# Splitting the first store of a rotary-embedding kernel: 2 KB rows first, then 30 KB rows

## Chip, cores, metric

One core of one Trainium2 chip. The metric is the device time in microseconds of that core.

## The reference

`x` is float32 of shape (8, 8, 1024, 64); `positions` has 1024 entries, `freqs` 32, `scale` is 0.5.

```python
half = x.shape[-1] // 2
angles = np.outer(positions * scale, freqs)
cos, sin = np.cos(angles), np.sin(angles)
x_first, x_second = x[..., :half], x[..., half:]
out = concatenate([x_first * cos - x_second * sin,
                   x_first * sin + x_second * cos], axis=-1)   # float32
```

Input and output are 16.8 MB each, and each is moved once.

## The kernel before

x is cut into NU = 4 units of 4 MB, each laid out as 128 partitions with one row of 32 KB (N = 8192 float32) in DRAM. GpSimd's DMA queue loads them with a cast to fp16, except for half of unit 0, of which Sync's and ScalarE's queues load a quarter each as float32. (In the code P = 128, NH = 4096 is half a row and Q = 2048 a quarter.) VectorE multiplies in fp16, ScalarE casts back to float32 into OUT, and the result is stored: units 0 and 1 in one 4 MB store each on GpSimd's queue, units 2 and 3 in halves on Sync's queue.

```python
xout = ctx.enter_context(tc.tile_pool(name="xout", bufs=3))
X0f = xout.tile([P, N], FP32, tag="O")
pin(nc.sync.dma_start(out=X0f[:, :Q], in_=xv[0][:, NH : NH + Q]))
# ... positions, freqs and the other quarter of unit 0 on the scalar queue (cut)
pin(nc.gpsimd.dma_start(out=Xf[0][:, :NH], in_=xv[0][:, :NH]))      # cast to fp16
# ... constants (cut)
for u in range(1, NU):
    pin(nc.gpsimd.dma_start(out=Xf[u], in_=xv[u]))                  # cast to fp16
# ... sin/cos tables: T (cut)
for u in range(NU):
    OUT = xout.tile([P, N], FP32, tag="O")
    for s in range(2):
        # ... ks, ns, sin_b, cos_b, pr (cut)
        pin(nc.vector.tensor_tensor(out=pr, in0=Xs, in1=sin_b, op=ALU.mult))
        pin(nc.vector.tensor_tensor(out=Xs, in0=Xs, in1=cos_b, op=ALU.mult))
        # ... subtract into the first half, add into the second half (cut)
        pin(nc.scalar.copy(out=OUT[:, ns], in_=Xf[u][:, ns]))
        if u >= NU // 2:
            pin(nc.sync.dma_start(out=ov[u][:, ns], in_=OUT[:, ns]))
    if u < NU // 2:
        pin(nc.gpsimd.dma_start(out=ov[u], in_=OUT))
```

Of the kernel before, what the change touches and what calls it, by code (L numbers as in the profile page):

```python
# [21 lines left out]
def kernel(  # L22
# [8 lines left out]
    nc = tc.nc  # L31
    pin = tc.keep_in_program_order
# [12 lines left out]
    K8 = S // P  # L45
    G = P // HP
    W = K8 * half
    assert S % HP == 0 and D == 2 * half and NBH % HEADS == 0 and G * K8 == K

    fscale = float(scale)  # L50
# [2 lines left out]
    ov = out.rearrange("b h s d -> (b h s d)").rearrange("(u p n) -> u p n", p=P, n=N)  # L53
# [34 lines left out]
        out=one, in_=one, compare_op=ALU.not_equal, fill=1.0, base=0,  # L88
        pattern=[[-1, G], [-G, HP]], channel_multiplier=1,
    ))  # L90
    for u in range(1, NU):
# [9 lines left out]
        out=posf, in_=pos_i64.bitcast(I32).rearrange("p (k t) -> p k t", t=2)[:, :, 0]  # L101
# [3 lines left out]
        out=y,  # L105
# [8 lines left out]
        out=r, in0=m, scalar=_MAGIC, in1=y, op0=ALU.subtract, op1=ALU.subtract  # L114
# [5 lines left out]
        out=ra.bitcast(I32), in0=r.bitcast(I32), scalar1=0x7FFFFFFF, scalar2=None, op0=ALU.bitwise_and  # L120
# [5 lines left out]
    for g in range(0, G, 2):  # L126
        ps = spread.tile([P, 2, 2, W], FP32, tag="g")
        for i in range(2):
            nc.tensor.matmul(  # L129
                out=ps[:, i].rearrange("p t w -> p (t w)"),  # L130
# [12 lines left out]
# [3 lines that stand above are left out]
            ks = slice(s * KH, (s + 1) * KH)  # L146
            ns = slice(s * NH, (s + 1) * NH)
            Xs = X[u][:, ks]
            sin_b = T[:, 0, ks].unsqueeze(2).broadcast_to((P, KH, 2, half))
            cos_b = T[:, 1, ks].unsqueeze(2).broadcast_to((P, KH, 2, half))  # L150
            pr = tmp.tile([P, KH, 2, half], FP16, tag="pr")
            pin(nc.vector.tensor_tensor(out=pr, in0=Xs, in1=sin_b, op=ALU.mult))  # L152
            pin(nc.vector.tensor_tensor(out=Xs, in0=Xs, in1=cos_b, op=ALU.mult))  # L153
            pin(nc.vector.tensor_tensor(  # L154
                out=Xs[:, :, 0, :], in0=Xs[:, :, 0, :], in1=pr[:, :, 1, :], op=ALU.subtract
            ))
            pin(nc.vector.tensor_tensor(  # L157
                out=Xs[:, :, 1, :], in0=pr[:, :, 0, :], in1=Xs[:, :, 1, :], op=ALU.add
            ))
            pin(nc.scalar.copy(out=OUT[:, ns], in_=Xf[u][:, ns]))  # L160
            if u >= NU // 2:
                pin(nc.sync.dma_start(out=ov[u][:, ns], in_=OUT[:, ns]))
        if u < NU // 2:
            pin(nc.gpsimd.dma_start(out=ov[u], in_=OUT))  # L164


# [33 lines left out]
```

## Time and profile before

| | before |
|---|---|
| time, median (lowest to highest, 6 runs) | 84.56 us (84.42 to 84.83) |
| span in the profile | 82.8 us |
| VectorE / ScalarE busy | 60.3 us / 40.1 us |
| bytes read and written in HBM | 16.79 + 16.78 MB |
| first DMA row to end of the last one | 79.76 us |

The utilisation slices and the chain of the kernel before are shown in the prediction.

One quantity is used throughout and is on no page. The trace keeps a record of each row that an engine moves (start, duration, bytes). A cast load row of 32 KB has a record of 1.227 us in the steady state. The **hole** is what the records of the load rows exceed their usual duration by, ahead of the first store row, as a mean over the 16 engines: 0.96 us before.

### The profile page before, as it was taken

To read this page: it belongs to the slowest core of one execution; us is meant where nothing else is said; L and a number is where in the kernel's file an instruction comes from. 1 tells how busy PE (TensorE), PEld (TensorE's weight loads), DVE (VectorE), ACT (ScalarE), POOL (GpSimd) and SP (SyncE) were. 2 spreads that over 40 slices of the span, in tenths; PEclk is the share of its full clock that TensorE was granted. 3 is DMA by queue.
4 is the path that set the end of the run, shared out by engine and by line. 5 is a ranking of instruction groups with operands and counts; after the bars stand their busy time and mean duration, and the time that the engine had idled before them with its cause. 6 is when DMAs were issued, how large, how long until landed. Compare 5 with 4: busy or idle time off the path is not lost.

```text
span 82.8 us, 179 instructions
## 1 busy us (share of the span) xinstructions
PE 7.0 (8%) x18; PEld 2.7 (3%) x18; DVE 60.3 (73%) x40; ACT 40.1 (49%) x18; POOL 4.6 (6%) x14
## 2 busy tenths in 40 slices
PE   0011799200000000000000000000000000000000
PEld 0011233000000000000000000000000000000000
DVE  0306276999999999999999999999999997000000
ACT  0602159999960690294088049209606912950000
POOL 4920000000000002000000200000000000000000
PEclk9999999975555555555555555555555555555555
DMA  2899998997999899699979989999899999999991
GB/s 40 335 326 269 293 333 182 253 238 150 246 253 198 182 253 238 143 253 253 127 301 459 507 348 412 507 443 420 380 436 420 412 420 436 444 420 436 428 428 55
DMA packets 1874, 26.22 MB, mean 317 GB/s; under 512 B 338, under 2 KB 338, under 8 KB 338
## 3 DMA queue, kind: packets, MB, share of 16 engines
q0 software_dynamic: 864, 15.73, 66.4%
q1 hardware_dynamic: 720, 9.44, 27.2%
q10 hardware_dynamic: 290, 1.06, 3.2%
HBM read 16.79 MB, written 16.78 MB: 406 GB/s over the span
## 4 chain that ended last, share of the span: by engine, by line
DVE 55%; ACT 14%; issue 6%; DMA 6%; PE 5%; DVEq 1%; ACTq 0%
DVE pr L152 19%; DVE X L153 19%; DVE X L157 9%; DVE X L154 6%; DMA freq_row<-in_freqs_dram 6%; ACT T L139 5%; ACT OUT L160 4%; PE ps L129 4%; ACT X L140 4%; DVEq L195 1%; PE cfreq L97 1%; ACT tab L122 1%; DVE r L113 1%; DVE y L104 1%; ACTq L69 0%
## 5 line engine op out<-in xcount | busy, mean ns | idle before, releaser
L160 ACT CAST OUT<-X 128x4096 f32<-128x4096 f16 x8 | 28.8, 3606 | 24.2 <-DVE X L157 24.2
L152 DVE TENSOR_TENSOR pr<-X,T 128x4096 f16<-128x4096 f16 x8 | 18.3, 2292 | 1.0 <-ACT T L139 0.7
L153 DVE TENSOR_TENSOR X<-X,T 128x4096 f16<-128x4096 f16 x8 | 18.3, 2292 | 0.3
L154 DVE TENSOR_TENSOR X<-X,pr 128x2048 f16<-128x2048 f16 x8 | 9.8, 1225 | 0.3
L157 DVE TENSOR_TENSOR X<-pr,X 128x2048 f16<-128x2048 f16 x8 | 9.7, 1219 | 0.0
L139 ACT CAST T<-ps 128x1024 f16<-128x1024 f32 x6 | 5.7, 1030 | 2.6 <-PE ps L129 2.6
L129 PE MATMUL ps<-tab,sel 128*128 128x512 f16 x16 | 6.4, 584 | 2.2 <-ACT tab L122 2.2
L137 DVE CAST T<-ps 128x1024 f16<-128x1024 f32 x2 | 2.5, 1225 | 2.2 <-PE ps L129 2.2
L140 ACT CAST X<-X0f 128x4096 f16<-128x4096 f32 x1 | 3.7, 3651 | 0.0
L164 POOL DMA_DIRECT2D out_dram<-OUT x2 | 1.1, 536 | 40.3 <-ACT OUT L160 40.3
L95 DVE COPY sel<-one 128x2048 f16<-128x2048 f16 x1 | 0.7, 693 | 2.8 <-POOL one L87 2.8
L117 ACT ACTIVATE tab<-r 128x256 f16<-128x256 f32 x1 | 0.4, 416 | 4.3 <-DVE r L113 4.3
L129 PEld LDWEIGHTS <-sel 128*128 128x128 f16 x16 | 2.2, 138 | 6.0 <-issue 5.8
L117 ACT ACT_TABLE_LOAD x1 | 1.3, 1283 | 2.1 <-issue 2.1
L92 POOL DMA_DIRECT2D X<-in_x_dram x3 | 2.0, 658 | 0.0
L100 DVE CAST posf<-pos_i 128x8 f32<-128x8 int32 x1 | 0.2, 172 | 2.3 <-DMA pos_i<-in_positions_dram 2.3
L97 PE MATMUL cfreq<-freq_row,coef 1*128 1x32 f32 x2 | 0.6, 392 | 5.9 <-DMA freq_row<-in_freqs_dram 5.9
L104 DVE TENSOR_TENSOR y<-posf,cfreq 128x256 f32<-128x256 f32 x1 | 0.4, 422 | 0.5 <-PE cfreq L97 0.5
L83 POOL DMA_DIRECT2D X<-in_x_dram x1 | 0.7, 667 | 0.8 <-POOLq L181 0.8
L97 PEld LDWEIGHTS cfreq<-freq_row,coef 1*128 1x128 f32 x2 | 0.5, 305 | 5.8 <-issue 5.8
L122 ACT ACTIVATE tab<-ra,quarter 128x256 f16<-128x256 f32 x1 | 0.5, 507 | 0.0
L113 DVE SCALAR_TENSOR_TENSOR r<-m,y 128x256 f32<-128x256 f32 x1 | 0.4, 424 | 0.0
(10 smaller groups left out, 1.9 us busy)
## 6 DMA issues: line engine op xcount, KB each, us to landing
out_dram<-OUT POOLq DMA_DIRECT2D x2, 4096.0 KB, 20.8
out_dram<-OUT SPq DMA_DIRECT2D x4, 2048.0 KB, 11.6
X<-in_x_dram POOLq DMA_DIRECT2D x3, 2048.0 KB, 28.7
X0f<-in_x_dram SPq DMA_DIRECT2D x1, 1024.0 KB, 4.8
X<-in_x_dram POOLq DMA_DIRECT2D x1, 1024.0 KB, 11.7
X0f<-in_x_dram ACTq DMA_DIRECT2D x1, 1024.0 KB, 12.2
pos_i<-in_positions_dram ACTq DMA_DIRECT2D x1, 8.0 KB, 5.0
freq_row<-in_freqs_dram ACTq DMA_DIRECT2D x1, 0.1 KB
```

Of the source, the lines that this page charges most:

```text
L92: pin(nc.gpsimd.dma_start(out=Xf[u], in_=xv[u]))
L97: nc.tensor.matmul(out=cfreq, lhsT=coef, rhs=freq_row, start=True, stop=True)
L117: pin(nc.scalar.activation(out=tab[:, 0], in_=r, func=AF.Sin, bias=0.0, scale=-_TWO_PI_DN))
L129: nc.tensor.matmul(out=ps[:, i].rearrange("p t w -> p (t w)"), lhsT=sel[:, g + i].rearrange("s h q -> s (h q)"), rhs=tab.rearrange("s t k ...
L137: pin(nc.vector.tensor_copy(out=dst, in_=ps))
L139: pin(nc.scalar.copy(out=dst, in_=ps))
L140: pin(nc.scalar.copy(out=Xf[0][:, NH:], in_=X0f[:, :NH]))
L152: pin(nc.vector.tensor_tensor(out=pr, in0=Xs, in1=sin_b, op=ALU.mult))
L153: pin(nc.vector.tensor_tensor(out=Xs, in0=Xs, in1=cos_b, op=ALU.mult))
L154: pin(nc.vector.tensor_tensor(out=Xs[:, :, 0, :], in0=Xs[:, :, 0, :], in1=pr[:, :, 1, :], op=ALU.subtract))
L157: pin(nc.vector.tensor_tensor(out=Xs[:, :, 1, :], in0=pr[:, :, 0, :], in1=Xs[:, :, 1, :], op=ALU.add))
L160: pin(nc.scalar.copy(out=OUT[:, ns], in_=Xf[u][:, ns]))
```

## The change

The intent: let small rows be the first that are stored, when GpSimd's queue passes from loads to stores.

```diff
+    C1 = 512
...
         if u < NU // 2:
-            pin(nc.gpsimd.dma_start(out=ov[u], in_=OUT))
+            c = C1 if u == 0 else 0
+            if c:
+                pin(nc.gpsimd.dma_start(out=ov[u][:, :c], in_=OUT[:, :c]))
+            pin(nc.gpsimd.dma_start(out=ov[u][:, c:], in_=OUT[:, c:]))
```

## The prediction

> **What bounds the kernel now.** I read the page from the utilisation slices to the queues, and only then the chain that ended last, because the two disagree. The chain names VectorE and ScalarE; the slices say that the 16 DMA engines are never free:
>
> ```profile
> span 82.8 us, 179 instructions
> DVE  0306276999999999999999999999999997000000
> ACT  0602159999960690294088049209606912950000
> DMA  2899998997999899699979989999899999999991
> HBM read 16.79 MB, written 16.78 MB: 406 GB/s over the span
> DVE 55%; ACT 14%; issue 6%; DMA 6%; PE 5%; DVEq 1%; ACTq 0%
> ```
>
> VectorE is done in slice 34 of 40 and ScalarE in slice 36, but DMA runs at nine tenths to the last slice but one. The few sevens and sixes come from the way a row is booked in the slice in which it starts. 33.6 MB in 82.8 us is close to all that these engines give here, as the stretches show (us, busy time of five engines with counts, clock, DMA share, GB/s):
>
> ```profile
> 26.00:38.00 12.00, 0.00 (x0) 0.00 (x0) 11.83 (x8) 6.99 (x2) 0.54 (x1) 0.50 1.02 217
> 38.00:39.00 1.00, 0.00 (x0) 0.00 (x0) 1.00 (x1) 0.22 (x1) 0.00 (x0) 0.50 0.91 164
> 39.00:40.00 1.00, 0.00 (x0) 0.00 (x0) 0.97 (x2) 0.00 (x0) 0.00 (x0) 0.50 0.57 115
> 40.00:41.00 1.00, 0.00 (x0) 0.00 (x0) 1.00 (x2) 0.00 (x0) 0.00 (x0) 0.50 2.01 262
> 41.00:42.00 1.00, 0.00 (x0) 0.00 (x0) 0.97 (x2) 0.34 (x1) 0.00 (x0) 0.50 0.00 0
> 42.00:43.00 1.00, 0.00 (x0) 0.00 (x0) 1.00 (x1) 1.00 (x1) 0.00 (x0) 0.50 1.25 524
> 43.00:55.00 12.00, 0.00 (x0) 0.00 (x0) 11.83 (x8) 5.87 (x2) 0.53 (x1) 0.50 1.01 437
> 67.00:79.00 12.00, 0.00 (x0) 0.00 (x0) 2.78 (x3) 3.60 (x1) 0.00 (x0) 0.50 1.01 431
> ```
>
> Until about 40 us the queue loads x with a cast (217 GB/s of fp16 written means twice that read, 434); from 42 us it stores at 431 to 437. Both are the same ceiling, reached from the read side and then from the write side. The only hole is between them: no row starts between 41 and 42 us. The trace's records of single rows (a row is one partition's run; each engine moves 8 rows of a DMA) size it. Cast rows of 32 KB start every 1.209 us on an engine, averaged over the 16. The last two of unit 3 take 1.412 us (38.993 to 40.405) and 1.991 us (40.405 to 42.396, where the first store row starts). Their excess is 0.20 + 0.78 = 0.98 us, or 0.96 without the 0.02 us of a completion record. Between the loads of two units there is no such excess (20.830 to 22.059 is 1.229, completion record included), nor between the two 4 MB stores (50.875 to 52.090). After 42.05 us the records of one engine add up to 39.05 us and the last ends at 81.50: no more idle time. So a delay removed at the turn is a delay removed at the end.
>
> What stands next behind DMA is the last store. The chain in order of time ends, and the DMA queue's own waits read:
>
> ```profile
> 69.84 3.60 ACT OUT L160
> SPq L162 <- ACT OUT L160: 71.3, 4, 51.2
> SPq L195 <- DMA out_dram<-OUT: 7.6, 2, 4.8
> ```
>
> Its copy ends at 73.44 and its last row is recorded as moved at 81.49; it has landed at 81.86, and the span closes 0.9 us later. On idle DMA it would need about 1.0 us to start (the first load is issued at 0.74, its first row starts at 1.74), eight rows of 0.611 us each, 4.89 us, and 0.37 us from last row to landing: 73.5 + 1.0 + 4.9 + 0.4 = 79.8. So 2.1 us can be taken from DMA before compute sets the end.
>
> **What the Trainium skill says.** "DMA: Bandwidth & Descriptors", section "Issuing engines are not separate DMA queues": all DMAs, whoever issues them, run on the same 16 engines and interleave. The trace agrees: from 55.8 us rows of the GpSimd queue (1.213 us) and the Sync queue (0.611 us) alternate, and the sum stays at the ceiling. The same page, section "Measured (HBM→SBUF, 128 partitions, SWDGE, issued from GpSimd)", has 425 GB/s for 16 MB; the stretches here show 431 to 437. Its section "Latency and other measured facts" gives HBM access 0.2 us on average and 2 us at high load; a hole of 0.96 us lies between, but no view shows the latency itself. "Perfetto Trace Analysis", section "DMA Optimizations": DMAs below 2 KB have a significant overhead each, and splitting helps if the engines are generally idle. Here they are not idle, and 2 KB is the edge.
>
> **The change, part by part.**
> *Removed*: one GpSimd store of 128 rows of 32 KB (unit 0). *Added*: a store of 128 rows of 2 KB, 256 KB in all, and one of 128 rows of 30 KB. Bytes are the same. The 2 KB store reads columns of the first half only, so it waits for one copy and can be issued at 20.40 + 3.61 = 24.0 us instead of 31.5. This moves nothing: GpSimd's queue works in order, all three unit loads were put on it by 4.7 us, and they end at 42. Instruction order on VectorE, ScalarE, TensorE and Sync is the same in both builds; one copy of the last unit now waits for three DMAs instead of two, the new one long landed by then (unit 0's store lands at 52.7, that copy starts at 62.84).
> *Cost of the rows*: the records give 309, 611 and 1213 ns for 8, 16 and 32 KB, so 36.7 ns per KB and about 9 ns per row. Estimated from that, a 2 KB row takes 82 ns, a 30 KB row 1.14 us; eight of each make 0.66 + 9.12 = 9.78 us on an engine against 8 x 1.213 = 9.70. With one more completion record (0.009 us) the cost is +0.09 us, all on the path. GpSimd's further issue, 0.54 us, is off it: the descriptors are written at 24 to 32 us and used at 42.
> *Gain at the turn*: only the 0.96 us hole is there to be won. My reading of it: an engine reads ahead of what it writes. During loads the read side is the limit, so when it begins on the store's 32 KB rows before the load has ended, those bytes delay the load's last rows: 0.96 us x 27 KB per us is about 26 KB per engine, most of one row. If the engine takes in whole rows by number, small first rows let it take in little (two or three would be 4 to 6 KB, 0.15 to 0.22 us), and 0.7 to 0.8 us is saved; it stays saved, since reads and writes run at one rate afterwards. If it takes in bytes, eight rows of 2 KB are only 16 KB per engine, and it reads on into the 30 KB row: nothing is saved.
>
> The trace speaks rather for bytes, or for many rows. The Sync store is issued at 52.33; with 1.0 us to start it could move at 53.3, but its first row starts between 55.8 and about 57.2, some 2.4 us (two 32 KB rows, 64 KB) beyond the rest of a row in work. At the start, GpSimd's load is issued at 1.25, yet its first row starts at 4.79, after the last of Sync's 8 KB rows: there at least six small rows were already in hand. So I expect part of the hole at best.
>
> **The rivals.**
> 1. *Whole rows by number*: gain 0.7 to 0.8, less 0.09: 83.8 to 83.9. For it: the hole is nearly a row long, and lies just where this change acts. Against: the eight small rows in hand at the start.
> 2. *Bytes, or a fixed latency of turning from HBM reads to stores*: gain 0, cost 0.09: 84.6. For it: 64 KB in hand in both cases above.
> 3. *In between*: the read-ahead stops at the 16 KB of small rows, since a 30 KB row no longer fits; 26 - 16 = 10 KB, 0.36 us saved, less 0.09: 84.25.
> 4. *Small rows are slower than the fit*, or a second, shorter hole opens when reading turns to 30 KB rows: 0.2 to 0.5 us lost, 84.7 to 85.0. For it: the skill's warning on small DMAs; no row near 2 KB is in this trace.
> A compute-set end is no rival: 2.1 us of room against 0.96.
>
> **Range and chances.** Weights 0.35, 0.3, 0.2 and 0.15 on 83.85, 84.6, 84.25 and 84.85 give 84.3; I put 84.2, as one seldom writes such an edit without a hole in view. The range is rival 1 at its fullest with the runs' noise (84.42 to 84.83 before), 83.5, to rival 4, 84.8. Faster by 2% needs 1.69 us, more than the hole holds: 0.03. Slower by 2% needs eight small rows to cost 0.2 us more each: 0.02.
>
> **What would show it.** In the changed profile the stretch 40 to 43 us tells: under rival 1 the last two load rows take close to 1.21 us each and the first store row starts near 41.6; under rival 2 they take 1.4 and 2.0 as before and the first store row starts near 42.4. The small rows should take 80 to 90 ns, the 30 KB rows 1.14 us, and no gap should follow. From there the engines' work should add up to 39.1 us and run without idle time to the end; the time should move by what the start of the first store row moved, plus 0.09. VectorE and ScalarE should show the same times as before to 0.1 us. The prediction is wrong if the end moves without that start moving, if a new hole lies between the two stores, or if the end comes below 79.8 us in the trace.

## The result, and the profile after

84.56 us median (84.49 to 84.82, 6 runs), against 84.56 us before (84.42 to 84.83, 6 runs). The ratio is 1.0002, 95% interval 0.9978 to 1.0026: the same. Ratios here are the mean time of one kernel's runs over the mean of the other's of the same rounds, so they are not quite the ratio of the medians quoted. Executions over 1.5% slower than the fastest of the same kernel are left out of the means.

From the page of the changed kernel, the lines that answer to those of before, and three lines of its DMA issues (KB each, median us from issue to landing):

```profile
span 82.8 us, 181 instructions
...
DVE  0306376999999999999999999999999996000000
ACT  0603069999950790393097059119507903930000
...
DMA  3899997997999899799989999999999899999990
...
HBM read 16.79 MB, written 16.78 MB: 405 GB/s over the span
...
out_dram<-OUT POOLq DMA_DIRECT2D x1, 4096.0 KB, 20.8
out_dram<-OUT POOLq DMA_DIRECT2D x1, 3840.0 KB, 21.5
out_dram<-OUT POOLq DMA_DIRECT2D x1, 256.0 KB, 19.6
```

The small store takes 19.6 us to land for 256 KB: it was issued at 24.1 us and stood behind the loads until 42, as predicted. Now the stretches of the changed kernel around the turn (us; busy time of five engines with counts; clock; DMA share, which can pass 1 because a row is booked whole where it starts; GB/s):

```profile
26.00:38.00 12.00, 0.00 (x0) 0.00 (x0) 11.83 (x8) 7.18 (x2) 0.53 (x1) 0.50 1.02 217
38.00:39.00 1.00, 0.00 (x0) 0.00 (x0) 1.00 (x1) 0.03 (x1) 0.00 (x0) 0.50 0.85 147
39.00:40.00 1.00, 0.00 (x0) 0.00 (x0) 0.97 (x2) 0.00 (x0) 0.00 (x0) 0.50 0.67 131
40.00:41.00 1.00, 0.00 (x0) 0.00 (x0) 1.00 (x2) 0.00 (x0) 0.00 (x0) 0.50 1.93 262
41.00:42.00 1.00, 0.00 (x0) 0.00 (x0) 0.97 (x2) 0.53 (x1) 0.00 (x0) 0.50 0.01 4
42.00:43.00 1.00, 0.00 (x0) 0.00 (x0) 1.00 (x1) 1.00 (x1) 0.00 (x0) 0.50 1.25 514
...
43.00:55.00 12.00, 0.00 (x0) 0.00 (x0) 11.83 (x8) 5.68 (x2) 0.53 (x1) 0.50 1.01 437
```

The empty microsecond from 41 to 42 us is still there (4 GB/s against 0), and 437 GB/s follow at once. In the records: the last two load rows take 1.44 and 1.93 us, a hole of 0.92 us against 0.96; the store begins at 42.34 us on the mean of the engines, 42.40 before. After the turn, the records of an engine add up to 39.09 us against 39.05. So the change removed nothing and cost next to nothing.

### The profile page after: what moved, and what is told of

It is laid out like the page before. It is cut to its first block, busy times and chain, and to the rows that moved or that the text cites. A ratio compares the mean times of both kernels' runs of the same rounds, so it can differ in the third digit from the quotient of the medians.

```text
span 82.8 us, 181 instructions
## 1 busy us (share of the span) xinstructions
PE 6.8 (8%) x18; PEld 2.7 (3%) x18; DVE 60.3 (73%) x40; ACT 40.1 (48%) x18; POOL 5.2 (6%) x15
## 4 chain that ended last, share of the span: by engine, by line
DVE 55%; ACT 15%; issue 6%; DMA 5%; PE 5%; DVEq 1%; ACTq 0%
DVE X L154 19%; DVE pr L153 19%; DVE X L158 9%; DVE X L155 6%; DMA freq_row<-in_freqs_dram 5%; ACT T L140 5%; ACT OUT L161 4%; PE ps L130 4%; ACT X L141 4%; DVEq L199 1%; PE cfreq L98 1%; ACT tab L123 1%; DVE r L114 1%; DVE y L105 1%; ACTq L70 0%
## 5 line engine op out<-in xcount | busy, mean ns | idle before, releaser
L168 POOL DMA_DIRECT2D out_dram<-OUT x2 | 1.1, 532 | 20.2 <-ACT OUT L161 20.2
L167 POOL DMA_DIRECT2D out_dram<-OUT x1 | 0.6, 554 | 19.4 <-ACT OUT L161 19.4
## 6 DMA issues: line engine op xcount, KB each, us to landing
out_dram<-OUT POOLq DMA_DIRECT2D x1, 256.0 KB, 19.6
```

## The experiments

The question is why the hole does not care about the size of the rows, and what it is. Theories, as they came:

- **Rows by number**: an engine takes in a few rows ahead; small rows would shrink the hole.
- **Bytes read ahead because loads with a cast leave the write side idle** (the prediction's reading).
- **Fixed turn**: each turn from loads to stores costs about 0.96 us.
- **First touch**: the first write to the output costs it, once.
- **Lead**: reading from SBUF gets ahead of the loads still under way, once, and the pipeline keeps that lead until it runs empty.

Medians of "before" below are those of the same chip and rounds. Each hole is read from one trace.

### small4: four stores of 2 KB rows instead of one

```diff
-            pin(nc.gpsimd.dma_start(out=ov[u], in_=OUT))
+            edges = [0, 512, 1024, 1536, 2048, N] if u == 0 else [0, N]
+            for lo, hi in zip(edges, edges[1:]):
+                pin(nc.gpsimd.dma_start(out=ov[u][:, lo:hi], in_=OUT[:, lo:hi]))
```

> Unit 0's store as four stores of 2 KB rows (64 KB per engine) and one of 24 KB rows. The hole at the turn was 0.98 us before and 0.92 us after the change (excess of the last two load rows over 1.209 us, completion record included). Theory 'rows by number' (some 9 to 15 rows taken in ahead, so that eight small ones were too few): the hole shrinks below 0.5 us. Theory 'bytes' (about 26 KB per engine taken in ahead): it stays at 0.85 to 1.0, as 64 KB of small rows lie behind it. Theory 'fixed turn': stays too. Small rows 2 x 2 KB in one record of 159 ns as in the changed kernel, so the work after the turn grows by about 4 x 0.03 us; time within 0.3% of before unless the hole shrinks.

84.44 us (before 84.57), ratio 0.9973 (0.9930 to 1.0015): the same. The hole is 0.77 us. That is a little below the 0.85 that "bytes" expected and far from the 0.5 of "rows by number"; since single traces of kernels without small rows spread from 0.81 to 1.23 us (split_x3 0.81, sync_store0 0.84, before 0.96, two_turns 1.01, less_dve 1.23), nothing is read from the 0.08. 64 KB per engine in small rows leave the hole standing: rows by number falls.

### split_x3 and two_turns: does each turn cost?

split_x3 loads unit 3 in two halves, order unchanged. two_turns puts the second half behind unit 0's store, so that the queue turns to stores twice:

```diff
-        pin(nc.gpsimd.dma_start(out=Xf[u], in_=xv[u]))
+        if u < NU - 1:
+            pin(nc.gpsimd.dma_start(out=Xf[u], in_=xv[u]))
+        else:
+            pin(nc.gpsimd.dma_start(out=Xf[u][:, :NH], in_=xv[u][:, :NH]))
...
             pin(nc.gpsimd.dma_start(out=ov[u], in_=OUT))
+            if u == 0:      # split_x3 has this load right behind the first half instead
+                pin(nc.gpsimd.dma_start(out=Xf[NU - 1][:, NH:], in_=xv[NU - 1][:, NH:]))
```

> Control for two_turns: unit 3 is loaded by two DMAs of 16 KB rows (read side), order unchanged. Hole 0.8 to 1.0 us as before, 8 x 2 x 0.02 us more load work at most (16 KB rows 0.624 us against half of 1.209): time 84.5 to 84.9.

> Second half of unit 3 is loaded behind unit 0's store, so GpSimd's queue turns from loads to stores twice and once back. Theory 'fixed turn': each turn to stores costs 0.96 us and nothing is given back, so the time grows by about 0.9 us over split_x3. Theory 'read-ahead' (bytes read early while the read side is the limit; the write side pays them back whenever it turns to loads): two holes, but the turn back from store to load gives about as much back (its first load rows start and end some 0.5 to 1 us early against 0.6 us each), time within 0.2 us of split_x3.

split_x3: 84.67 us (before 84.57), ratio 1.0003 (0.9958 to 1.0047), hole 0.81. two_turns: 84.83 us, ratio 1.0015 (0.9974 to 1.0055). The 4 us ahead of its first turn and of its second, as stretches of two_turns (usual for loads: 217):

```profile
33.20:37.20 4.00, 0.00 (x0) 0.00 (x0) 3.93 (x3) 2.91 (x1) 0.00 (x0) 0.50 1.05 168
...
47.90:51.90 4.00, 0.00 (x0) 0.00 (x0) 3.93 (x3) 3.51 (x1) 0.00 (x0) 0.50 1.03 211
```

The first turn has a hole of 1.01 us, the second one of 0.12. Fixed turn falls. The expected giving back falls too: after the turn back to loads the first half rows start at 47.32 and 47.93 us on the mean of the engines, 0.61 us apart, their usual pace, and the first of them no earlier than the last store row's end (47.32). The cost came once and was not returned.

### f32_between: what changes at the turn?

```diff
+    extra = consts.tile([P, 2048], FP32)
+    pin(nc.gpsimd.dma_start(out=extra, in_=xv[0][:, :2048]))   # behind the loads, unused
```

> An uncast load of 128 rows of 8 KB, unused, between unit 3's load and unit 0's store. It adds 8 x 0.309 = 2.47 us of work per engine, and the time should grow by 2.4 to 2.5 us if DMA sets the end as predicted (a compute-set end would hide up to all of it). Where the hole is: if it comes of the change of limit from read to write (cast to plain), at the cast load's last rows, before the extra load; if it comes of the source changing from HBM to SBUF, at the last rows of the extra load, before the store.

86.96 us against 84.57, ratio 1.0278 (1.0237 to 1.0320): 2.35 us for 2.47 us of added DMA work. Its stretches: the end of the cast loads (37 to 41.8 us), then the extra load, then the store.

```profile
37.00:39.40 2.40, 0.00 (x0) 0.00 (x0) 2.33 (x2) 1.31 (x1) 0.00 (x0) 0.50 1.02 218
39.40:41.80 2.40, 0.00 (x0) 0.00 (x0) 2.37 (x3) 0.05 (x1) 0.00 (x0) 0.50 0.74 198
41.80:42.80 1.00, 0.00 (x0) 0.00 (x0) 1.00 (x1) 1.00 (x1) 0.00 (x0) 0.50 1.15 360
42.80:43.80 1.00, 0.00 (x0) 0.00 (x0) 1.00 (x1) 1.00 (x1) 0.00 (x0) 0.50 0.96 213
...
45.20:49.00 3.80, 0.00 (x0) 0.00 (x0) 3.73 (x4) 0.36 (x2) 0.53 (x1) 0.50 0.96 414
```

The extra load writes as many bytes as it reads, and falls to 213 GB/s in the middle of itself. In the records no cast row exceeds 1.227 us (the 198 comes of row starts that fall just ahead of the stretch), and the extra rows of 8 KB, 0.309 us each elsewhere, exceed that by 0.91 us in sum. So the hole stands before the first row whose source is SBUF, not where the casts end. It does not need cast rows ahead of it, and on these the prediction's reading rested.

### sync_store0: the first store on another queue

```diff
-            pin(nc.gpsimd.dma_start(out=ov[u], in_=OUT))
+            pin((nc.sync if u == 0 else nc.gpsimd).dma_start(out=ov[u], in_=OUT))
```

> Unit 0's store is issued on Sync's queue at about 31.5 us instead of GpSimd's, so its rows go in between unit 3's loads and no engine turns from loads to stores all at once. Theory 'fixed turn': with the rows mixed the single hole of 0.96 us vanishes or is spread, time 83.6 to 84.0. Theory 'read-ahead': the bytes read early only move; time within 0.2 us of before, 84.4 to 84.7. In both, unit 3's landing moves from 43 to about 51 us, still ahead of its first use at 55.75 us.

85.06 us against 84.57, ratio 1.0060 (1.0043 to 1.0077). The hole did not vanish; it moved with the first store row, to 32.9 to 36.2 us in the middle of the loads, and is 0.84 us:

```profile
32.00:36.00 4.00, 0.00 (x0) 0.00 (x0) 3.97 (x3) 1.62 (x1) 0.00 (x0) 0.50 0.84 139
```

From there a load row and a store row alternate, five loads and six stores, each at 1.226 us, without any further loss. That the kernel is 0.6% slower (0.5 us) comes from the end of the program, not from the rows: they take 79.54 us from first to last (79.76 before), but 1.32 us pass from the last landing to the end of the span instead of 0.90. These 0.43 us or so recur in every run that puts one more DMA on Sync's queue; where they lie is shown under early_tiny below. (The profiled run, 84.75 us, is the fastest of the six; why others reach 85.24 no trace shows.)

### less_dve: is compute the bound after all?

```diff
+            if u == 0:          # wrong result on purpose
-            pin(nc.vector.tensor_tensor(
-                out=Xs[:, :, 1, :], in0=pr[:, :, 0, :], in1=Xs[:, :, 1, :], op=ALU.add
-            ))
+                pin(nc.vector.tensor_tensor(
+                    out=Xs[:, :, 1, :], in0=pr[:, :, 0, :], in1=Xs[:, :, 1, :], op=ALU.add
+                ))
```

> Wrong result on purpose: the last of the four VectorE operations of each half is left out for units 1 to 3 (6 x 1.15 us less on VectorE, so the last copy and the last store are ready about 6.9 us earlier). If DMA sets the end, as predicted, the time stays within 0.3 us of before; if the chain of compute sets it, the time falls by 2 us or more.

84.69 us against 84.57, ratio 1.0016 (0.9996 to 1.0036). The last pieces of its chain in order of time (start, us, what):

```profile
61.30 1.24 DVE X L154
62.56 3.60 ACT OUT L161
```

Before, the last copy began at 69.84 us; here it begins 7.3 us earlier, and the time does not fall. Compute is not what sets the end. (The hole is 1.23 us in this trace, the largest with an unchanged turn. Its load rows are also uneven earlier, by 0.18 us in sum among those that start between 17 and 30 us, which the trace of the kernel before does not show.)

### early_tiny, early_16k, early_big, early_sbuf: an SBUF read during the loads

Each adds one DMA on Sync's queue behind the first load; the columns written are written again by the last store.

```diff
+    pin(nc.sync.dma_start(out=ov[NU - 1][:, :16], in_=X0f[:, :16]))    # early_tiny
+    pin(nc.sync.dma_start(out=ov[NU - 1][:, :512], in_=X0f[:, :512]))  # early_16k
+    pin(nc.sync.dma_start(out=ov[NU - 1][:, :Q], in_=X0f[:, :Q]))      # early_big
+    spare = consts.tile([P, Q], FP32)                                  # early_sbuf
+    pin(nc.sync.dma_start(out=spare, in_=X0f[:, :Q]))                  # early_sbuf
```

> One extra store of 128 rows of 64 B (512 B per engine) from an input buffer to columns that the last store writes again, issued on Sync at about 5.5 us, in the middle of the loads. So far the hole appeared once, at the first row that is read from SBUF and written to HBM, and not again at later turns. Theory 'first touch' (the first write to the output costs some 0.9 us once, whatever its size): no hole of more than 0.2 us at 40 to 42 us, it lies at 6 to 9 us instead or is lost among the start. Theory 'lead' (an engine's reading gets ahead of its writing by some 26 KB of stores once, and keeps that lead): 512 B build no lead, the hole at 40 us stays at 0.85 to 1.0 us. Time within 0.3% of before in both unless the start hides it (then up to 0.9 us less).

> The same extra store with 128 rows of 8 KB (64 KB per engine). Work +8 x 0.309 = 2.47 us. Both theories: the hole of 0.8 to 1.0 us moves to 6 to 12 us, and at 40 to 46 us less than 0.2 us is left; time +2.4 to +2.6 us. If the hole at the later turn is full, both fall, and the cost belongs to each turn out of a long run of loads.

> The same 64 KB per engine copied from SBUF to SBUF instead of to HBM. If reading from SBUF is what overtakes the loads (theory 'lead'): the hole moves to 6 to 12 us and less than 0.2 us is left at the turn to stores. If writing to HBM is what costs: the hole stays at the turn, 0.85 to 1.0 us. Time +2.4 to +2.6 us either way.

> The early extra store with 128 rows of 2 KB, 16 KB per engine: between 512 B (hole at the turn stayed, 0.85 us) and 64 KB (hole 0.06 us). Theory 'lead' in bytes: the early store builds a lead of at most 16 KB, so of the hole 0.96 - 16/27 = about 0.37 us is left at 40 to 42 us (0.2 to 0.55). If it takes a whole large row to build it: 0.85 or more is left. If any store of full-size descriptors settles it: under 0.1. Work +8 x 0.08 = 0.65 us, time +0.5 to +0.7 us.

| run | extra bytes per engine | excess of load rows before 15 us | hole at the turn | time (before) | ratio, 95% interval |
|---|---|---|---|---|---|
| early_tiny | 512 B to HBM | 0.04 us | 0.85 us | 84.98 (84.63) | 1.0039, 1.0010 to 1.0069 |
| early_16k | 16 KB to HBM | 0.02 us | 0.76 us | 85.51 (84.48) | 1.0122, 1.0099 to 1.0145 |
| early_big | 64 KB to HBM | 0.47 us | 0.06 us | 86.99 (84.63) | 1.0275, 1.0250 to 1.0299 |
| early_sbuf | 64 KB to SBUF | 0.59 us | 0.00 us | 86.97 (84.63) | 1.0274, 1.0250 to 1.0298 |

The 4 us ahead of the first row of unit 0's store, for early_tiny, then early_big, then early_sbuf:

```profile
38.00:42.00 4.00, 0.00 (x0) 0.00 (x0) 3.93 (x4) 0.56 (x2) 0.00 (x0) 0.50 0.88 143
```

```profile
40.30:44.30 4.00, 0.00 (x0) 0.00 (x0) 3.93 (x4) 1.42 (x1) 0.00 (x0) 0.50 0.97 213
```

```profile
40.40:44.40 4.00, 0.00 (x0) 0.00 (x0) 3.93 (x4) 1.28 (x1) 0.00 (x0) 0.50 0.96 213
```

143 GB/s with the hole, 213 without. A tiny write to the output does not remove it: first touch falls. A copy that writes nothing to HBM removes it: the source in SBUF is what matters. That it is not just 64 KB more on a second queue, the kernel before shows: ScalarE's queue brings in eight rows of 8 KB per engine from HBM among the cast loads, from 5 to 12 us, and the hole comes all the same. Two expectations of "lead" missed. early_16k should have left 0.37 us and left 0.76, nearer to the 0.85 that a lead built by whole large rows asked for. Why is open: its 2 KB rows alternated one by one with load rows, but so did the 8 KB rows of early_big. And the cost that early_big and early_sbuf pay early, 0.47 and 0.59 us, is less than the hole they save.

The times of all four hold 0.43 us that have nothing to do with the hole. From the last landing to the end of the span 1.32 or 1.33 us pass in these four, in early_big_gap, prelead and sync_store0, all with one more DMA on Sync's queue, and 0.89 or 0.90 in the others. The semaphore instructions of the program's end show it (count, ns, first and last start), before and in early_tiny:

```profile
L195 SPq EVENT_SEMAPHORE  x10: 17/28/28, 73.9 to 82.7; - x10
L196 SPq EVENT_SEMAPHORE  x10: 17/28/28, 81.9 to 83.2; - x10
```

Sync waits for all DMAs one after another. Before, the last store (landed at 81.86 us) stands last in that list, and the other waits are over by then; in early_tiny it (81.88) stands first, and seven waits follow it, 0.06 us each. With this early_16k adds up to 1.00 us (0.77 for its rows, 0.43 for the end, 0.20 less hole) against 1.03 measured, and early_tiny to some 0.5 against 0.35. It also means that early_big and early_sbuf came near the expected time only because two terms cancelled. f32_between adds as many rows of the same size, keeps its hole and is 2.35 us slower; early_big is 2.33 us slower with 0.43 us of it at the end. So its rows alone cost about 1.9 us, and some 0.4 us of the hole was really saved (an estimate, as the end was read in one trace of each kernel).

### early_big_gap: does it last through idle engines?

As early_big, with the loads of units 2 and 3 issued only when unit 0's output is ready:

```diff
-    for u in range(1, NU):
-        pin(nc.gpsimd.dma_start(out=Xf[u], in_=xv[u]))
+    pin(nc.gpsimd.dma_start(out=Xf[1], in_=xv[1]))
...
+            if u == 0:
+                gate = consts.tile([P, 1], FP32)
+                pin(nc.gpsimd.tensor_copy(out=gate, in_=OUT[:, N - 1 : N]))
+                for v in range(2, NU):
+                    pin(nc.gpsimd.dma_start(out=Xf[v], in_=xv[v]))
             pin(nc.gpsimd.dma_start(out=ov[u], in_=OUT))
```

> As early_big, but the loads of units 2 and 3 are held back until unit 0's output is ready (about 31 us), so that the DMA engines run empty for some 8 us between the early store and the turn to stores. Theory 'lead' (a state of a running pipeline): it is lost when the engines run empty, so the hole is back at the turn (about 52 us), 0.75 to 1.0 us. Theory 'once' (a one-time cost of the first sizeable SBUF read, whatever follows): the hole stays under 0.15 us as in early_big. The time is longer by some 8 to 11 us either way and says nothing.

One look, 99.34 us (state unknown, and the time is not compared). Two stretches of it: the idle time, and the 4 us ahead of its turn to stores.

```profile
26.00:34.00 8.00, 0.00 (x0) 0.00 (x0) 7.86 (x6) 3.60 (x1) 1.29 (x2) 0.50 0.00 0
...
52.00:56.00 4.00, 0.00 (x0) 0.00 (x0) 3.93 (x4) 2.59 (x1) 0.00 (x0) 0.50 1.02 184
```

The engines moved nothing for 8 us, and the hole is back, with 1.09 us in the records (its last row alone takes 2.20 us instead of 1.23). A one-time cost falls; the state that was bought by the early store is lost when the engines run empty. This is what "lead" asked for. It is one trace, but the 1.09 us stand far from the 0.06 of early_big.

### prelead: paying while the engines wait for the first load

```diff
+    seed = consts.tile([P, 1024], FP32)
+    spare = consts.tile([P, 1024], FP32)
+    pin(nc.vector.memset(seed, 0.0))
+    pin(nc.sync.dma_start(out=spare, in_=seed))
     pin(nc.sync.dma_start(out=X0f[:, :Q], in_=xv[0][:, NH : NH + Q]))
```

> A try to build the lead when the DMA engines wait for the first load anyway: 32 KB per engine (128 rows of 4 KB) copied from SBUF to SBUF, issued on Sync ahead of the first load. If the lead is built then and lasts through 40 us of loads: hole under 0.2 us at the turn, 0.96 us less, against 8 x 0.16 = 1.28 us more work, of which up to 0.5 us lies in the wait for the first rows: time -0.2 to +0.4 us. If a lead needs loads in flight to overtake, or is lost while the first loads start from nothing: hole 0.8 us or more, time +0.8 to +1.3 us.

94.80 us against 84.48, ratio 1.1220 (1.1196 to 1.1244): neither expectation, and a useless test. Its list of who waited for whom shows why (us in total, times, longest):

```profile
ACT X L144 <- DMA X0f<-in_x_dram: 14.8, 1, 14.8
DVE pr L156 <- ACT X L144: 12.9, 1, 12.9
```

The copy waited for the memset and came to Sync's queue after GpSimd's loads, so the small rows of both Sync DMAs got their turns between load rows of 0.62 to 1.23 us. The quarter of unit 0 that Sync loads took 26.4 us to land instead of 4.8, and VectorE stood still for 12.9 us. The first store was issued at 43.6 us and its first rows started at 44.8, when the loads had ended (44.3 at the latest), so that no load row was left to be delayed. No version faster than both kernels came out.

## Why the prediction was right, and where its steps failed

- **DMA is the bound**: held. Less VectorE work changed nothing (1.0016); 2.47 us more DMA work cost 2.35 us.
- **Only the hole is there to be won, so 2% is out of reach**: held.
- **Rows cost 82 ns at 2 KB, 1.14 us at 30 KB, +0.09 us in all**: nearly. (Its 36.7 ns per KB are for KB of 1000 bytes, its row sizes KB of 1024; the row times come out right.) The 30 KB rows take 1.138 us. The trace has one record of 4 KB and 159 ns for two 2 KB rows, 80 ns each, and the whole grew by 0.04 us.
- **The early issue moves nothing**: held (19.6 us from issue to landing). Its sign that VectorE and ScalarE keep their times to 0.1 us was missed by a little, and off the path: the first copy starts at 20.22 us, 20.40 before.
- **Gain at the turn**: this step failed. The prediction gave 0.55 of its weight to rivals 1 and 3, which win 0.36 to 0.8 us, and put 84.2. Rival 2 came: no gain, 84.6 predicted, 84.56 measured. The shift of the hole, 0.96 to 0.92 us, is well inside the spread of 0.81 to 1.23 us over five traces without small rows. That the measured time lies in the stated range is owed to the range, which reached over a gain, no gain and a loss; its centre rested on a gain that did not come. small4 shows why: 64 KB per engine in 2 KB rows left a hole of 0.77 us. What the prediction itself said against rivals 1 and 3, that many small rows were already in hand elsewhere in the trace (at least six by its reading, eight in its list of rivals), deserved the greater weight.
- **Why the hole is there**: half right. That store bytes get ahead of load bytes fits all runs that could decide. That they do so because cast loads leave the write side idle is wrong as a condition: in f32_between the hole stands in uncast rows, 0.91 us. What the runs show is: the cost arises when rows from SBUF come in behind or between rows from HBM, with first rows of 2 KB or of 32 KB at the turn and with 8 KB among the loads, on either queue, to HBM or to SBUF, but not with early stores of 512 B or 16 KB per engine (0.04 and 0.02 us); it comes once (0.12 us at the second turn of two_turns, nothing in the alternation of sync_store0); and it comes again when the engines have run empty. That it is bytes sitting in a buffer is inferred: no view shows a buffer, and the one test of its size in bytes (early_16k) missed.

What stays open: whether the 0.9 us can be saved in a faster kernel. early_big and early_sbuf saved some 0.4 us of it by the estimate above, but with 2.5 us of added work; an early read from SBUF that is of use in itself was not tried.

## What to carry to other kernels

When the DMA digits are near 9 to the end, look in the records for the places where rows take longer than their usual time, and size them before touching anything: their sum is the most that any reordering can win. A gap in front of a DMA need not depend on that DMA's shape; ask whether it comes once or at each such place by making a second one. And a row that enters a busy queue behind large rows waits for its turns: prelead lost 10 us by delaying a small load on which all compute depended. And look at the end of the program too: one more DMA on a queue changed the order of the last waits and cost 0.43 us, which looked like a cost of the rows.

## What the Trainium skill lacked or had wrong

- The cost of the first SBUF-sourced rows after HBM loads: in none of the pages read for this. Here 0.76 to 1.23 us per engine, once, 0.00 to 0.12 us at a later turn while the engines stay busy, and 1.09 us again after 8 us of idling.
- "DMA: Bandwidth & Descriptors", section "Queues, rings and completion order", says that an engine round-robins between its queues at packet granularity, a packet being typically 9 to 17 descriptors. Here two running queues alternated single rows (32 KB and 16 KB, from 57 us on); which rows make a packet no view shows. It has no figure for how long a newly filled queue waits for its first turn: the first Sync store rows started 3.5 to 4.9 us after their issue, by the prediction's estimate 2.5 to 3.9 us after they could have moved.
- The same page, section "Where 436 GB/s comes from", has about 358 GB/s, half of a stack's 716, binding for transfers between HBM and SBUF; that this is with both cores of a pair streaming, the page says only beside its 425 GB/s for one core. This core, the only one that the program uses, held 418 to 437 GB/s over 12 us stretches of stores (418 where two queues alternate); 425 is the figure to go by.
